# One DMA queue for loads and stores of a batched matmul: six batches loaded first, then stores and loads in turns of two

## The chip, the cores and the metric

The kernel runs on one core of a Trainium2 chip. The metric is the time of one execution in device microseconds (us). The runs of one comparison were made on one chip, in alternating rounds. A ratio is the mean time of one kernel's runs over that of the other's runs of the same rounds, so it is not quite the ratio of the medians that stand beside it.

## The reference

```python
# x: 16 x 768 x 512, y: 16 x 768 x 1024, float32
def reference(x, y):
    return np.einsum('bkm,bkn->bmn', x, y).astype(np.float32)
```

For each of 16 batches, 1.573 MB of x and 3.146 MB of y come in and 2.097 MB go out. That is 109.05 MB in all, each byte moved once.

## The kernel before

SyncE issues every transfer on one queue. Two staging buffers (`xs`, `ys`) take a batch's x and y as float32. VectorE casts them to bf16 (`xb`, `yb`), TensorE multiplies into two halves of PSUM, and ScalarE copies the result into one of five output buffers (`ob`), from which it is stored. The order on the queue is the matter of this document:

```python
    LAG = 4
    NO = 5
    ...
    def store(b):
        if b < B - 2:
            nc.sync.wait_ge(groups, 2 * (b + 2))       # TensorE has finished batch b + 1
        else:
            nc.sync.wait_ge(outs, b - (B - 3))         # ScalarE has copied batch b
        nc.sync.dma_start(o_v[b], ob[b % NO][:]).then_inc(so[b % NO], 16)

    for b in range(B):
        i = b % 2
        if b >= 2:
            nc.sync.wait_ge(cast, nx[b - 2])           # xs[i] has been cast
        wide_dma("x", xs[i][:], x_v[b], 4, True).then_inc(sx[i], 16)
        if b >= 2:
            nc.sync.wait_ge(cast, nx[b - 2] + parts(b - 2))   # ys[i] has been cast
        wide_dma("y", ys[i][:], y_v[b], 2, True).then_inc(sy[i], 16)
        if b >= LAG:
            store(b - LAG)
    for b in range(B - LAG, B - 1):
        store(b)
    ...
    # ScalarE, before it copies batch b into ob[b % NO]:
        if b >= NO:
            nc.scalar.wait_ge(so[b % NO], 16 * (b // NO))     # store b - 5 has landed
    ...
    nc.sync.dma_start(o_v[B - 1], ob[(B - 1) % NO][:])        # the last store, after the section
```

(Comments added; the rest is cut.) Below, x5, y5 and S5 are batch 5's loads and its store. The order of before is x0 y0 ... x4 y4, S0, x5 y5, S1, x6 y6, and so on to y15, S11, and then S12 to S15. I call a move from loads into stores a switch (turn or excursion); before has 12, the last of them into the stores that end the program.

Of the kernel before, what the change touches and what calls it, by code (L numbers as in the profile page):

```python
# [1 line left out]

_os.environ.setdefault("NEURON_RT_ULTRASERVER_MODE", "4")

# [2 lines left out]

# [5 lines left out]


@with_exitstack
def kernel(
    ctx: ExitStack,
    tc: tile.TileContext,
    x: bass.AP,
    y: bass.AP,  # L20
    out: bass.AP,
):
    nc = tc.nc
    P = 128
    FP32 = mybir.dt.float32
    BF16 = mybir.dt.bfloat16

    B, K, M = x.shape
    _, _, N = y.shape
    KT = K // P  # L30
    MT = M // P
    NF = 512
    NT = N // NF



    x_v = x.rearrange("b (p ko) m -> b p ko m", ko=KT)
    y_v = y.rearrange("b (p ko) n -> b p ko n", ko=KT)
    o_v = out.rearrange("b (p mo) n -> b p mo n", mo=MT)

    LAG = 4
    NO = 5
    KH = KT // 2

    section = ExitStack()
    section.enter_context(tc.tile_critical())
    ec = ctx.enter_context
    xs = [ec(nc.sbuf_tensor(f"xs{i}", [P, KT, M], FP32)) for i in range(2)]
    ys = [ec(nc.sbuf_tensor(f"ys{i}", [P, KT, N], FP32)) for i in range(2)]
    xb = ec(nc.sbuf_tensor("xb", [P, 2, KT, M], BF16))  # L50
    yb = ec(nc.sbuf_tensor("yb", [P, 2, KT, N], BF16))
    ob = [ec(nc.sbuf_tensor(f"ob{i}", [P, MT, N], FP32)) for i in range(NO)]

    HB = MT // 2
    ps = [ec(nc.psum_tensor(f"ps{i}", [P, HB, NT, NF], FP32)) for i in range(2)]
    sx = [ec(nc.semaphore(f"sx{i}")) for i in range(2)]
    sy = [ec(nc.semaphore(f"sy{i}")) for i in range(2)]
    so = [ec(nc.semaphore(f"so{i}")) for i in range(NO)]
    cast = ec(nc.semaphore("cast"))
    ready = ec(nc.semaphore("ready"))  # L60
    room = ec(nc.semaphore("room"))
    groups = ec(nc.semaphore("groups"))
    idle = ec(nc.semaphore("idle"))
    outs = ec(nc.semaphore("outs"))


    made = {}

    def wide_dma(key, dst, src, dram_rows, load):


        if key not in made:
            made[key] = nc.sync.dma_start(dst, src)
            return made[key]
        pat = mybir.BassSymbolicTensorAccessPattern
        widen = lambda a: a.rearrange("(q r) k m -> q (r k m)", r=dram_rows)
        plain = lambda a: a.rearrange("p k m -> p (k m)")
        s, d = (widen(src), plain(dst)) if load else (plain(src), widen(dst))
        return nc.sync.add_instruction(_copy.replace(
            made[key].ins, name=nc.get_next_instruction_name(),  # L80
            ins=(pat(ap=s.ap, dtype=s.dtype, bass_ap=s, is_dma=False),),
            outs=(pat(ap=d.ap, dtype=d.dtype, bass_ap=d, is_dma=False),),
            sync_info=None, ant_dge_precooked=False))


    def parts(b):
        return 2 if b in (15,) else 1


    nx = [sum(1 + parts(a) for a in range(b)) + 1 for b in range(B)]  # L90


    def store(b):


        if b < B - 2:
            nc.sync.wait_ge(groups, 2 * (b + 2))
        else:
            nc.sync.wait_ge(outs, b - (B - 3))
        nc.sync.dma_start(o_v[b], ob[b % NO][:]).then_inc(so[b % NO], 16)  # L100

    for b in range(B):
        i = b % 2
        if b >= 2:
            nc.sync.wait_ge(cast, nx[b - 2])
        wide_dma("x", xs[i][:], x_v[b], 4, True).then_inc(sx[i], 16)
        if b >= 2:
            nc.sync.wait_ge(cast, nx[b - 2] + parts(b - 2))
        wide_dma("y", ys[i][:], y_v[b], 2, True).then_inc(sy[i], 16)
        if b >= LAG:  # L110
            store(b - LAG)
    for b in range(B - LAG, B - 1):
        store(b)


    for _ in range(60):
        nc.vector.sem_inc(idle, 1)
    for b in range(B):
        i = b % 2
        n = 16 * (b // 2 + 1)  # L120
        if b >= 2:
            nc.vector.wait_ge(groups, 2 * (b - 1))
        nc.vector.wait_ge(sx[i], n)
        nc.vector.tensor_copy(xb[:, i], xs[i][:]).then_inc(cast, 1)  # L124
        nc.vector.wait_ge(sy[i], n)
        for h in range(parts(b)):
            ks = slice(h * KT // parts(b), (h + 1) * KT // parts(b))
            nc.vector.tensor_copy(yb[:, i, ks], ys[i][:, ks]).then_inc(cast, 1)  # L128


    for b in range(B):
        nc.gpsimd.wait_ge(cast, nx[b]).then_inc(ready, 1)
        for h in range(parts(b)):
            nc.gpsimd.wait_ge(cast, nx[b] + h + 1).then_inc(ready, 2 // parts(b))


    x_w = xb[:].rearrange("p s k (j mo) -> p s k mo j", mo=MT)
    pe = OrderedEngineSet([nc.tensor.engine])
    with nc.Fori(0, B // 2, engines=pe):
        with nc.Fori(0, 2, engines=pe) as s:  # L140
            nc.tensor.wait_ge(ready, 2).then_inc(ready, -2)
            for mo in range(MT):
                g, m = divmod(mo, HB)
                if m == 0:
                    nc.tensor.wait_ge(room, 1).then_inc(room, -1)  # L145
                for kt in range(KT):
                    if mo == 0 and kt == KH:
                        nc.tensor.wait_ge(ready, 1).then_inc(ready, -1)
                    for nt in range(NT):
                        mm = nc.tensor.matmul(  # L150
                            ps[g][:, m, nt], x_w[:, bass.ds(s, 1), kt, mo],
                            yb[:, bass.ds(s, 1), kt, nt * NF:(nt + 1) * NF],
                            start=(kt == 0), stop=(kt == KT - 1))
                if m == HB - 1:
                    mm.then_inc(groups, 1)


    nc.scalar.nop().then_inc(room, 2)
    for _ in range(60):
        nc.scalar.sem_inc(idle, 1)  # L160
    for b in range(B):
        if b >= NO:
            nc.scalar.wait_ge(so[b % NO], 16 * (b // NO))
        for g in range(2):
            nc.scalar.wait_ge(groups, 2 * b + g + 1)
            cp = nc.scalar.copy(ob[b % NO][:, g * HB:(g + 1) * HB].rearrange("p m (t f) -> p m t f", f=NF),  # L166
                                ps[g][:])
            if b < B - 1:
                cp.then_inc(room, 1)
        if b == B - 2:  # L170
            nc.scalar.drain().then_inc(outs, 1)
    cp.then_inc(outs, 1)

    for b in range(B - LAG - 1, B - 2):
        nc.sync.wait_ge(so[b % NO], 16 * (b // NO + 1))
    section.close()




    nc.sync.dma_start(o_v[B - 1], ob[(B - 1) % NO][:])


# [1 line left out]
_INS = ['x', 'y']  # L185
_OUTS = [((16, 512, 1024), 'float32')]


# [23 lines left out]
```

## Time and profile before

| | before |
|---|---|
| time, median of the first 3 runs | 261.9 us (261.72 to 262.05) |
| span in the profile | 260.7 us |
| busiest compute engine | TensorE, 71% |
| queue: share of 16 engines' span | 98.1% |
| bytes over span | 418 GB/s |

The profile's page gives busy time as a share of the span, and a row of 40 equal slices in tenths. Here the row "DMA" is the one that matters, since it stands at 8 or 9 nearly throughout. Where a load landed is best read from VectorE in the timeline: its cast of y starts as soon as the y load's semaphore is full. The columns of such a line are start (us), duration (us), engine, source line, operation, tiles, shapes, and in brackets the idle time ahead and what ended it. The prediction shows these lines.

### The profile page before, as it was taken

How to read it: one execution, taken by the hardware profiler on the slowest of the kernel's cores; microseconds unless marked ns; L12 is line 12 of the kernel's file. 1: busy time of each engine (PE TensorE's matmuls, PEld its weight loads, DVE VectorE, ACT ScalarE, POOL GpSimd, SP SyncE). 2: the span in 40 equal slices, each digit the busy share in tenths (PEclk: the TensorE clock that was granted, in tenths of full speed). 3: DMA queues.
4: the chain of work that ended last, by engine and by line, in shares of the span. 5: the costliest groups of instructions: out<-in, count | busy, mean ns of one | idle time of the engine just before them, and what ended most of it. 6: DMA issues, size and time to landing. Idle time of an engine off the chain costs nothing. (4 is left out here: it accounts for less than half of the span.)

```text
span 260.7 us, 2506 instructions
## 1 busy us (share of the span) xinstructions
PE 186.1 (71%) x768; PEld 89.8 (34%) x768; DVE 82.0 (31%) x33; ACT 61.1 (23%) x33; POOL 0.2 (0%) x4
## 2 busy tenths in 40 slices
PE   0009999998937949479596894969959197696910
PEld 0004555554512515124242351434425043253500
DVE  0261644525222252312524115252142522225000
ACT  1000442243220222202214022040322205022220
POOL 0000000000000000000000000000000000000000
PEclk9999999999995999959889797797999889799985
DMA  7998999999899899989999989999998999999994
GB/s 260 432 494 385 468 385 468 392 392 488 385 410 493 370 450 475 427 385 405 483 400 437 465 367 453 410 483 402 410 485 382 445 468 417 410 410 430 427 410 181
DMA packets 4514, 109.07 MB, mean 418 GB/s; under 512 B 768, under 2 KB 768, under 8 KB 768
## 3 DMA queue, kind: packets, MB, share of 16 engines
q1 hardware_dynamic: 4512, 109.05, 98.1%
q14 instruction: 2, 0.02, 0.0%
HBM read 75.50 MB, written 33.55 MB: 418 GB/s over the span
## 5 line engine op out<-in xcount | busy, mean ns | idle before, releaser
L150 PE MATMUL ps<-yb,xb 128*128 x768 | 186.1, 407 | 62.7 <-PEq L145 60.7
L150 PEld LDWEIGHTS ps<-yb,xb 128*128 x768 | 89.8, 117 | 158.5 <-issue 92.2
L166 ACT COPY ob<-ps 128x2048 f32<-128x2048 f32 x32 | 59.8, 1870 | 184.2 <-PE ps L150 184.2
L128 DVE CAST yb<-ys 128x6144 bf16<-128x6144 f32 (+1 forms) x17 | 53.8, 3171 | 87.7 <-DMA ys<-in_y_dram 87.7
L124 DVE CAST xb<-xs 128x3072 bf16<-128x3072 f32 x16 | 28.2, 1760 | 69.4 <-DMA xs<-in_x_dram 65.3
L166 ACT ACT_TABLE_LOAD x1 | 1.3, 1283 | 5.3 <-issue 5.3
L196 POOL MEMSET const-bfloat16-1.0<- 128x1 bf16 x1 | 0.1, 102 | 0.0
L196 POOL MEMSET const-uint8-127<- 128x1 uint8 x1 | 0.1, 102 | 0.0
L196 POOL MEMSET const-float32-1.0<- 128x1 f32 x1 | 0.1, 99 | 0.0
L196 POOL MEMSET const-float32-0.0<- 128x1 f32 x1 | 0.1, 98 | 0.2 <-issue 0.2
## 6 DMA issues: line engine op xcount, KB each, us to landing
ys<-in_y_dram SPq DMA_DIRECT2D x16, 3072.0 KB, 28.2
out_dram<-ob SPq DMA_DIRECT2D x16, 2048.0 KB, 32.6
xs<-in_x_dram SPq DMA_DIRECT2D x16, 1536.0 KB, 29.7
```

Source lines behind the costliest of these rows:

```text
L124: nc.vector.tensor_copy(xb[:, i], xs[i][:]).then_inc(cast, 1)
L128: nc.vector.tensor_copy(yb[:, i, ks], ys[i][:, ks]).then_inc(cast, 1)
L150: mm = nc.tensor.matmul(ps[g][:, m, nt], x_w[:, bass.ds(s, 1), kt, mo], yb[:, bass.ds(s, 1), kt, nt * NF:(nt + 1) * NF], start=(kt == 0), ...
L166: cp = nc.scalar.copy(ob[b % NO][:, g * HB:(g + 1) * HB].rearrange("p m (t f) -> p m t f", f=NF), ps[g][:])
L196: nc = _bacc.Bacc("TRN2", target_bir_lowering=False, num_devices=1)
```

## The change

It is meant to alternate less often between reading and writing the memory, and to have more loads ahead of the compute engines at the start. Six batches are loaded before the first store. Then two stores and two loads take turns.

```diff
-    LAG = 4
+    FIRST = 6
+    TURN = 2
     NO = 5
...
-    for b in range(B):
+    def load(b):
         i = b % 2
         ...            # x and y of batch b, with the same waits
-        if b >= LAG:
-            store(b - LAG)
-    for b in range(B - LAG, B - 1):
+
+    for b in range(B):
+        load(b)
+        if b + 1 >= FIRST and (b + 1 - FIRST) % TURN == 0:
+            a = b + 1 - FIRST
+            for c in range(a, a + TURN):
+                store(c)
+    for b in range(B - FIRST + TURN, B - 1):
         store(b)
...
-    for b in range(B - LAG - 1, B - 2):
+    for b in range(B - NO, B - 2):      # the same range, 11 to 13
         nc.sync.wait_ge(so[b % NO], 16 * (b // NO + 1))
```

The order is then x0 y0 ... x5 y5, S0 S1, x6 y6 x7 y7, S2 S3, ..., x14 y14 x15 y15, S10 S11, S12 to S15: 6 switches, 5 of them among the loads.

## The prediction

> **What bounds the kernel now.** I read the page first, then the queue's own waits, then VectorE's line in the timeline, because VectorE starts a cast as soon as a load has landed and so marks the landings.
>
> ```profile
> span 260.7 us, 2506 instructions
> PE 186.1 (71%) x768; PEld 89.8 (34%) x768; DVE 82.0 (31%) x33; ACT 61.1 (23%) x33; POOL 0.2 (0%) x4
> ...
> DMA  7998999999899899989999989999998999999994
> ...
> q1 hardware_dynamic: 4512, 109.05, 98.1%
> ...
> PE 9%; ACT 1%; issue 0%
> ...
> ys<-in_y_dram SPq DMA_DIRECT2D x16, 3072.0 KB, 28.2
> out_dram<-ob SPq DMA_DIRECT2D x16, 2048.0 KB, 32.6
> xs<-in_x_dram SPq DMA_DIRECT2D x16, 1536.0 KB, 29.7
> ```
>
> No compute engine is over 71%. The one queue is busy 98.1% of the span, in nearly every slice. The chain that ended last accounts for only 10% of the span: it follows instructions and stops where a transfer is the releaser, so it is no guide here. A transfer of 2 to 3 MB needs some 5 to 7 us but lands 28 to 33 us after its issue: about 21 to 28 us of it is standing in line behind others. The queue is never short of work in the steady part.
>
> The queue's own waits (where the issuing engine stands still):
>
> ```profile
> SPq L73 <- DVE yb L128: 117.0, 14, 9.1
> SPq L73 <- DVE xb L124: 66.7, 14, 6.0
> SPq L100 <- PE ps L150: 28.2, 4, 15.9
> ```
>
> The issuer waits 184 us for casts that free the two staging buffers. That looks like a bound and isn't one: with 28 us between issue and landing, these waits run while earlier transfers move.
>
> VectorE in the timeline; a line with "yb<-ys" starts where a batch's y has landed (first column, us):
>
> ```profile
> 26.19 3.36 DVE L128 CAST yb<-ys 128x6144 bf16<-128x6144 f32 x1 [5.54 <-DMA ys<-in_y_dram]
> ...
> 37.18 3.36 DVE L128 CAST yb<-ys 128x6144 bf16<-128x6144 f32 x1 [3.86 <-DMA ys<-in_y_dram]
> ...
> 48.18 3.36 DVE L128 CAST yb<-ys 128x6144 bf16<-128x6144 f32 x1 [4.49 <-DMA ys<-in_y_dram]
> ...
> 188.27 3.36 DVE L128 CAST yb<-ys 128x6144 bf16<-128x6144 f32 x1 [5.45 <-DMA ys<-in_y_dram]
> 196.85 1.76 DVE L124 CAST xb<-xs 128x3072 bf16<-128x3072 f32 x1 [5.23 <-DMA xs<-in_x_dram]
> 204.06 3.36 DVE L128 CAST yb<-ys 128x6144 bf16<-128x6144 f32 x1 [5.45 <-DMA ys<-in_y_dram]
> ...
> 219.89 3.36 DVE L128 CAST yb<-ys 128x6144 bf16<-128x6144 f32 x1 [5.46 <-DMA ys<-in_y_dram]
> 228.48 1.76 DVE L124 CAST xb<-xs 128x3072 bf16<-128x3072 f32 x1 [5.23 <-DMA xs<-in_x_dram]
> 235.70 3.43 DVE L128 CAST yb<-ys 128x3072 bf16<-128x3072 f32 x2 [5.46 <-DMA ys<-in_y_dram]
> ```
>
> Three readings. (1) From an x landing to its y landing lie 7.21 us (196.85 to 204.06): 3.146 MB at 436 GB/s. (2) Batches 1 to 3 come with no store among them: 10.99 and 11.00 us for 4.719 MB. (3) Batches 12 to 15 come with one store each: 15.79, 15.83 and 15.81 us, mean 15.81, for 6.816 MB. The difference, 15.81 less 11.00, is 4.81 us for the 2.097 MB of a store: again 436 GB/s. **A store put between two loads costs its own bytes and nothing for the turn from reading to writing and back.**
>
> **What the Trainium skill says.** "DMA: Bandwidth & Descriptors", section "Where 436 GB/s comes from", gives 16 ports x 32 B x 850 MHz = 435.2 GB/s as the ceiling of the core's path; the trace agrees (436 in readings 1 and 3). The same page, section "Two DMAs through the same engine are not ordered", says that descriptors of one queue start in order but are pipelined, and that an engine's read and write sides are separate queues. That fits a turn that costs nothing: the next descriptor need not wait for the last to be written. "HBM Reference", section "Access", puts a core that streams alone at about 425 GB/s, bounded by its 16 DMA engines; here 418 is the mean over the span with its start and end. No page I read gives a cost for alternating loads and stores.
>
> **The change part by part.** The bytes stay: 16 x (1.573 + 3.146 + 2.097) = 109.05 MB, at 436 GB/s 250.2 us. The last store was issued at 250.88 and landed after 9.0 us (the minimum among the stores), at 259.9: 9.7 us above the floor. Where those lie, from landing less bytes so far over 436 GB/s: 4.5 us at batch 1 (start-up and first latency), 4.9 at batch 3, 8.2 at batch 8 (124.86 less 116.7), 9.5 at batch 15. So 4.5 us belong to the start, 3.3 came between batches 3 and 8, and the rest is 0.17 us a batch, which is in the store-free batches too (11.00 less 10.83), so it isn't a turn.
>
> Turns: before, stores 0 to 10 lie singly among the loads, 11 excursions. After, stores 0 to 9 lie in five pairs: six excursions fewer. By the difference of readings 2 and 3 each is worth 4.81 - 2.097/0.436 = 0.00 us, and the spread of the steady batches is 0.04 us. Gain: 6 x 0.00, at most 6 x 0.04 = 0.2 us. If I charged the whole 0.17 us to the turn, 1.0 us.
>
> Loads early: y4 and x5 are issued as before, since each waits for the cast two batches back (y5 at 48.18 + 3.36 = 51.5, as now). Store 0 now moves behind y5 rather than ahead of x5. So y5 should land 4.8 us earlier than its present 76.28, near 71.3, and the stores 0 and 1 about 76 and 81. The queue doesn't run dry: y5 is cast at about 74.8 and y7 issued then, while most of store 0, store 1, x6, y6 and x7 (together 9.6 + 3.6 + 7.2 + 3.6 = 24 us of bytes) are still ahead of it. In the pairs that follow, between a y and the y that takes its buffer lie two x, one y and two stores, 10.5 MB or 24 us, as now; the cast and issue take about 4.
>
> Output buffers: ScalarE's copy for an odd batch b now needs store b-5, which stands directly behind y of batch b. It lands 4.8 us after that y. ScalarE needs it after the cast (3.4) and half of TensorE's batch (5.2, the spacing of the copies in the timeline), 8.6 us after that y. Slack 3.8 us, no wait.
>
> Tail: after y15 now come stores 10 to 15 rather than 11 to 15. y15 should land 4.8 us earlier, near 230.9. Behind it are 6 x 4.81 = 28.9 us of stores: 259.8, where the end is now. Store 15 must be issued some 2 us before store 14 has moved (about 255). TensorE takes batch 14 from 223.8 as now (y14 has the same bytes ahead of it), ends it near 236, goes straight on with 15 (before, it began at 238.03) and ends near 247; ScalarE's copy near 249, and the issue comes after store 13's landing near 250. In time; and a last store issued sooner is worth nothing while store 14 is still moving.
>
> Sum: turns 0 to -0.2, loads early 0, buffers 0, tail 0.
>
> **The rivals.** A: turns are dear. Then the pairs save up to the 1.0 us above (260.9), and if all that slipped after batch 3 (4.6 us) were due to alternation, halving it would give 2.3 us: 259.6. Against it: the 0.7 us lost between y3 (48.18) and y4 (59.71) fell before any store had moved; the steady batches lose nothing. B: a new wait. Bunched stores could let the staging buffers starve or ScalarE stall on an output buffer, each pair then opening a hole of 1 to 2 us in the queue, five times: 267 to 272. For it: the slack for the odd batches is 3.8 us, where before a store stood a whole batch ahead of its reuse. Against it: the 28 us of standing in line, and that a late ScalarE first eats into TensorE's idle time (62.7 us), not the queue's. C: the irregular losses, 3.3 us between batches 3 and 8, move. They have no cause that the views show, and a different order of reads and writes meets them differently: about 1 us either way. D: the tail with compute on the path. Were y15's compute what sets the end, 4.8 us would be saved; but the stores behind it move at full rate to the end, so the earlier landing is paid back in full by the extra store behind it.
>
> **Range and chances.** I predict 261.8 us: the 261.9 of before less 0.1. The spread of before is 0.3 us; rival C gives about 1 us either way, A up to 2 us down, B is unlikely. Range 260.3 to 263.2. Faster by 2% means below 256.7: it would take all of the 4.6 us that slip after batch 3 and more; 2 in 100. Slower by 2% means above 267.1: rival B in each pair; 4 in 100. Within 2%: 94 in 100.
>
> **What would show it.** Right: the queue's busy share stays near 98%; from one odd batch's y landing to the next odd one's about 31.6 us (twice 15.81), with 11.0 us inside a pair and 20.6 across two stores; y15's cast begins near 231 rather than 235.7; the last store is issued near 250 and the span ends near 260.6. Wrong by A: less than 31.4 us for a pair of batches, and an end before 259. Wrong by B: slices of DMA below 9 in the middle, ScalarE waiting for a store, stores landing much later than 38 us after issue. Wrong by D: an end that follows y15's landing down.

## The result, and the profile after

| | before | after |
|---|---|---|
| median, 4 runs each | 261.98 us (261.72 to 262.17) | 261.6 us (261.33 to 261.67) |
| ratio, after over before | | 0.9984, 95% interval 0.9967 to 1.0002 |
| span in the profile | 260.7 us | 259.9 us |

The verdict is "same", and the range on record held it. The page of the changed kernel has the same picture as before:

```profile
span 259.9 us, 2506 instructions
...
DMA  7998999999999998999999999999999999999994
...
q1 hardware_dynamic: 4512, 109.05, 98.3%
...
ys<-in_y_dram SPq DMA_DIRECT2D x16, 3072.0 KB, 28.3
out_dram<-ob SPq DMA_DIRECT2D x16, 2048.0 KB, 32.7
xs<-in_x_dram SPq DMA_DIRECT2D x16, 1536.0 KB, 29.8
```

The queue's share rose from 98.1% to 98.3%, and the times from issue to landing (last column, us) moved by 0.1 us each. The queue was full before and is full after. VectorE's casts of y in the timeline of the changed kernel show the new rhythm:

```profile
25.89 3.36 DVE L135 CAST yb<-ys 128x6144 bf16<-128x6144 f32 x1 [5.54 <-DMA ys<-in_y_dram]
...
58.87 3.36 DVE L135 CAST yb<-ys 128x6144 bf16<-128x6144 f32 x1 [4.53 <-DMA ys<-in_y_dram]
...
70.48 3.36 DVE L135 CAST yb<-ys 128x6144 bf16<-128x6144 f32 x1 [5.78 <-DMA ys<-in_y_dram]
...
91.21 3.36 DVE L135 CAST yb<-ys 128x6144 bf16<-128x6144 f32 x1 [5.48 <-DMA ys<-in_y_dram]
...
102.20 3.36 DVE L135 CAST yb<-ys 128x6144 bf16<-128x6144 f32 x1 [5.47 <-DMA ys<-in_y_dram]
...
122.87 3.36 DVE L135 CAST yb<-ys 128x6144 bf16<-128x6144 f32 x1 [5.47 <-DMA ys<-in_y_dram]
...
133.86 3.36 DVE L135 CAST yb<-ys 128x6144 bf16<-128x6144 f32 x1 [5.47 <-DMA ys<-in_y_dram]
...
229.42 3.43 DVE L135 CAST yb<-ys 128x3072 bf16<-128x3072 f32 x2 [5.47 <-DMA ys<-in_y_dram]
```

These are y1, y4 to y9, and y15. Inside a pair, y6 to y7, lie 10.99 us; across two stores, y7 to y8, lie 20.67 us, of which 20.67 - 10.99 = 9.68 us, or 4.84 each, belong to the stores. y15 is cast at 229.42, not 235.70: 6.3 us earlier. The end came only 0.8 us earlier. One more store stands behind y15, which takes back 4.8 us, and the stretch from y15's cast to the end took 0.7 us more beyond its stores (25.0 us for five stores before, 30.5 us for six after). The last issues of the two kernels, in the timeline of SyncE, before and after:

```profile
250.88 0.33 SPq L181 DMA_DIRECT2D out_dram<-ob  x1
```

```profile
249.97 0.33 SPq L188 DMA_DIRECT2D out_dram<-ob  x1
```

Two lines of detail bear on what was wrong in the prediction. In before, y4 and y5 were cast at these times:

```profile
59.71 3.36 DVE L128 CAST yb<-ys 128x6144 bf16<-128x6144 f32 x1 [5.67 <-DMA ys<-in_y_dram]
...
76.28 3.36 DVE L128 CAST yb<-ys 128x6144 bf16<-128x6144 f32 x1 [6.18 <-DMA ys<-in_y_dram]
```

Before, y3 to y4 took 59.71 - 48.18 = 11.53 us, 0.54 more than the 10.99 of a batch without a store. After, it took 10.99, and y4 to y5 took 70.48 - 58.87 = 11.61. The long step moved with the first store. y4 before and y5 after are each the load just ahead of it. In the records of single DMA packets, the first packet of S0 began at 57.7 us in before, 2.0 us ahead of y4's cast, and at 68.9 in after, 1.6 us ahead of y5's. So the long load was still under way when the first store began.

**A measure for the experiments.** Two steady figures, 10.99 us for a batch's loads and 15.81 - 10.99 = 4.82 us for a store, account for a queue that loses nothing. (The 4.82 us includes a switch, but stores in longer rows cost no less: 4.84 us each in rows of two, above, and in the rows of three and four below. So a settled switch costs nothing that shows.) I call slip what the stretch from y1's cast to y15's takes beyond 14 x 10.99 + 4.82 for each store that stands ahead of y15. For before: 235.70 - 26.19 - 153.86 - 11 x 4.82 = 2.6 us. For after: 229.42 - 25.89 - 153.86 - 10 x 4.82 = 1.5 us. If switches cost nothing anywhere, slip has no reason to depend on the order. Slip ends at y15, so what is lost behind y15 is not in it.

**Where the slip sits.** The records of single DMA packets in the trace also show it. Each transfer ends with 16 completion writes, one for each DMA engine. Their times for the first load and the last store, in us, worked out from those records:

```
                    first load: earliest, latest    last store: earliest, median, latest
before                   6.3     6.9                    256.6   256.7   259.5
after                    6.1     6.8                    256.2   256.8   258.6
```

Most of the 16 engines end together. In before three end 0.8 to 1.4 us behind the median and one 2.8 us; in after the last two end 1.3 and 1.8 us behind it. A transfer counts as landed only when the last has written. The lag grows on the way: the last write came 0.8 us behind the median at y1 and 3.0 at y15 in before, 0.6 and 1.3 in after. In before, the records that ran long are nearly all packets of a y load just ahead of a store: 0.2 to 0.7 us long on nearly all engines at the first switch, later mainly on the engine that lags (0.8, 0.7 and 0.6 us at three of the next four switches) and less on the others. So what the change could touch is the long load at the first switch and the lag of the slowest engine.

### The profile page after: what moved, and what is told of

It is laid out like the page before. It is cut to its first block, busy times and chain, and to the rows that moved or that the text cites. A ratio compares the mean times of both kernels' runs of the same rounds, so it can differ in the third digit from the quotient of the medians.

```text
span 259.9 us, 2506 instructions
## 1 busy us (share of the span) xinstructions
PE 178.8 (69%) x768; PEld 88.8 (34%) x768; DVE 82.0 (32%) x33; ACT 61.1 (24%) x33; POOL 0.2 (0%) x4
## 3 DMA queue, kind: packets, MB, share of 16 engines
q1 hardware_dynamic: 4512, 109.05, 98.3%
## 5 line engine op out<-in xcount | busy, mean ns | idle before, releaser
L157 PE MATMUL ps<-yb,xb 128*128 x768 | 178.8, 397 | 65.8 <-PEq L152 65.8
L157 PEld LDWEIGHTS ps<-yb,xb 128*128 x768 | 88.8, 116 | 155.4 <-issue 84.0
L173 ACT COPY ob<-ps 128x2048 f32<-128x2048 f32 x32 | 59.8, 1870 | 180.1 <-PE ps L157 180.1
```

Source lines behind the costliest of these rows:

```text
L157: mm = nc.tensor.matmul(ps[g][:, m, nt], x_w[:, bass.ds(s, 1), kt, mo], yb[:, bass.ds(s, 1), kt, nt * NF:(nt + 1) * NF], start=(kt == 0), ...
L173: cp = nc.scalar.copy(ob[b % NO][:, g * HB:(g + 1) * HB].rearrange("p m (t f) -> p m t f", f=NF), ps[g][:])
```

## The experiments

The theory (theory 1): the queue is always full, switches are free, the bytes set the time. Its rivals: switches cost (theory 2), or the new order starves ScalarE or the buffers (rival B). Seven kernels, and the change once more, ran on one chip; four runs that those results led to followed on another. All results were correct except those of the two kernels that do no compute. Medians of before were 261.97, 262.52 and 262.23 us.

### One part alone: six loads first, stores singly

```diff
-    LAG = 4
+    LAG = 5
```

> The six loads come first, then stores singly: the change without its pairs (10 excursions into stores among the loads, where before has 11 and the pairs have 5). Theory 1, of the prediction: turns are free and the queue is full throughout, so within 0.3 us of before (261.6 to 262.3) and y15 is cast near 230. Theory 2, formed from the two traces: the last y ahead of a store is lengthened, by 0.5 to 0.6 us at the first turn and by little or nothing later. Then the long step moves to y5: y3 to y4 takes 11.0 us (11.53 before), y4 to y5 about 11.6, as in the kernel with pairs; the time is 261.7 to 262.1. Rival B (ScalarE or buffers starve with the store so close to its reuse): over 263.

Measured: 261.74 us, ratio to before 0.9992 (0.9979 to 1.0005). y15 was cast at 229.82. y3 to y4 took 11.00 and y4 to y5 11.86 us, so the long step moved to the load ahead of the first store, as expected of theory 2. The slip was 1.8 us. Rival B has no support: ScalarE waited for no store. The early loads, with one store fewer ahead of y15, are worth nothing that the interval can tell from zero.

### Fewer switches: three by three

```diff
-    FIRST = 6
-    TURN = 2
+    FIRST = 7
+    TURN = 3
```

> Seven loads first, then three stores and three loads in turns: 3 excursions among the loads instead of 5 or 11. With five output buffers ScalarE must now wait for stores (batch 5 needs store 0, which stands behind y6). Theory 1: ScalarE and TensorE wait up to 7 us per turn, but from idle time, the queue never runs dry, turns are free: 261.3 to 262.0. Theory 2 (turns cost a little): 0.1 to 0.3 us below the pairs, 261.2 to 261.6. Rival B: the new ScalarE waits reach the queue; over 263.

Measured: 260.84 us, ratio 0.9957 (0.9945 to 0.9970); on the other chip, below, 0.9952. This is lower than any theory had it. The slip fell to 0.6 us. The waits show at the same time that ScalarE now stands still for stores (columns: us in all, times, longest):

```profile
ACT ob L173 <- PE ps L157: 141.7, 24, 20.3
...
ACT ob L173 <- DMA out_dram<-ob: 35.5, 4, 10.8
```

35.5 us of new waiting, and the kernel is faster. The waits replace idle time that ScalarE spent on TensorE (180.1 us in the changed kernel, 141.7 here). Rival B's mechanism exists and doesn't reach the queue.

### Halves of stores, together and apart

The control issues the two halves of each of stores 0 to 14 one after the other; the test puts one half behind x and one behind y.

```diff
-        nc.sync.dma_start(o_v[b], ob[b % NO][:]).then_inc(so[b % NO], 16)
+        for h in range(2):
+            nc.sync.dma_start(o_v[b][:, 2 * h:2 * h + 2],
+                              ob[b % NO][:, 2 * h:2 * h + 2]).then_inc(so[b % NO], 16)
...            # the waits on so count 32 for a store, not 16
```

> Each of stores 0 to 14 of the kernel before is issued as two halves one right after the other: the same 11 excursions, with packets of 8 KB instead of 16 KB. It is the control for the next run. A packet of 8 KB took 307 to 309 ns in the trace of before and one of 16 KB 611, so 16 engines' share grows by some 15 x 8 x 5 ns = 0.6 us at most plus the extra completion writes: 262.0 to 262.9 under each theory.

Measured: 262.53 us, ratio to before 1.0023 (1.0010 to 1.0036): the price of smaller packets, within what was expected (two packets of 8 KB took 2 x 309 ns in this trace, where one of 16 KB took 611 in before). The test, shown against the control:

```diff
         wide_dma("x", xs[i][:], x_v[b], 4, True).then_inc(sx[i], 16)
+        if b >= LAG:
+            store(b - LAG, (0,))
         if b >= 2:
             nc.sync.wait_ge(cast, nx[b - 2] + parts(b - 2))
         wide_dma("y", ys[i][:], y_v[b], 2, True).then_inc(sy[i], 16)
         if b >= LAG:
-            store(b - LAG)
+            store(b - LAG, (1,))
...            # store() takes the halves to issue as an argument
```

> The same halves, but one behind x and one behind y: 23 excursions instead of 11 or 12. Against the control of halves issued together. Theory 1 (turns free): within 0.3 us of that control. Theory 2 (a turn costs a little, 0.05 to 0.2 us each on the slowest of the 16 engines): 0.5 to 2 us above it. Rival A (0.17 us a turn in full): about 2 us above it. If the turn costs only after a y load and not after an x load: as theory 1.

Measured: 261.68 us, ratio to before 0.9995 (0.9981 to 1.0010), so 0.85 us below its control by the medians, where every theory had it level or above. Twice as many switches cost nothing; they even went with less slip (1.6 against 2.6 us, by the same measure). A fixed price per switch, theory 2 as I had put it, is refuted by this pair. Of the 1.6 us, 1.3 came at the first switch (y3 to y4 took 14.67 us, where 10.99 and half a store make 13.40); the 22 later switches took 0.3.

### The changed kernel again

> The changed kernel once more, in five rounds against before on this chip. Each theory: 0.1 to 0.6 us below before. If the difference is only which engine happened to be hit in one trace, it goes to zero; if turns cost, it stays near 0.4 us.

Measured: 261.85 us against 262.52 of before in the same rounds, ratio 0.9974 (0.9961 to 0.9986). The gain is small but clear of zero here. This trace's slip was 2.0 us, against 1.5 in the first, so single traces of one kernel differ by half a microsecond.

### No compute

TensorE's and ScalarE's work is taken out, and the five output buffers are filled with zeros once. VectorE still casts and so still paces the loads.

```diff
-        if b < B - 2:
-            nc.sync.wait_ge(groups, 2 * (b + 2))
-        else:
-            nc.sync.wait_ge(outs, b - (B - 3))
+        nc.sync.wait_ge(outs, NO)
...
-        if b >= 2:
-            nc.vector.wait_ge(groups, 2 * (b - 1))
...            # all of TensorE's and ScalarE's loops removed
+    for t in ob:
+        nc.gpsimd.memset(t[:], 0.0).then_inc(outs, 1)
```

> Wrong results on purpose: TensorE and ScalarE do nothing, the stores write zeros from buffers filled once, VectorE casts as before and paces the loads; order of the kernel before. Theory 1: the queue alone sets the time, so 261 to 262, and the batch steps are those of before (11.0 us without a store, 15.8 with one). If the slips between batches 3 and 8 come from compute that uses the on-chip memory beside the transfers: they vanish and the time falls by 2 to 3 us to 259 or 260.

Measured: 262.19 us, ratio to before 0.9992 (0.9979 to 1.0005). Without any matmul the kernel takes the same time, which is the plainest proof that, in this order, the queue alone sets it. The slip is there too, 2.5 us; y3, y4 and y5 in VectorE's timeline of this kernel:

```profile
48.02 3.36 DVE L123 CAST yb<-ys 128x6144 bf16<-128x6144 f32 x1 [5.54 <-DMA ys<-in_y_dram]
...
59.74 3.36 DVE L123 CAST yb<-ys 128x6144 bf16<-128x6144 f32 x1 [6.27 <-DMA ys<-in_y_dram]
...
75.61 3.36 DVE L123 CAST yb<-ys 128x6144 bf16<-128x6144 f32 x1 [5.56 <-DMA ys<-in_y_dram]
```

59.74 - 48.02 = 11.72 us: the long step ahead of the first store needs no TensorE or ScalarE beside it.

> The same without compute in the order of the changed kernel. Theory 1 (turns free): as the one before, within 0.2 us. Theory 2 (turns cost on the slowest engine): 0.3 to 0.6 us below it, as with compute. If the small gain of the pairs comes from compute moved in time, there is none here.

Measured: 261.21 us, ratio to before 0.9952 (0.9938 to 0.9965); by the medians 1.0 us below the run without compute in the order of before, more than expected. Its slip was 1.9 us. So the small gain of the pairs is there without compute, and belongs to the transfers. With compute the pairs took 261.85 us in the same rounds, 0.6 more than without: in this order compute costs a little after all, and no run here shows where.

### The other direction: four loads first

```diff
-    LAG = 4
+    LAG = 3
...
-    for b in range(B - LAG - 1, B - 2):
+    for b in range(B - NO, B - 2):
```

> The opposite direction: single stores, begun one load earlier (12 excursions among the loads). y15 has one more store ahead of it and should land 4.8 us later, near 240.5. From y15's landing to the issue of the last store before took 15.2 us (235.70 to 250.88), so it is issued near 255.7 and lands 7 to 9 us after, while store 14 ahead of it has moved by 255: compute comes onto the path and the time is 264 to 266. If the queue alone set the end (theory 1 taken without its limit): 262. Theory 2 on the first turn: the long step moves to y3: y2 to y3 about 11.5 us, y3 to y4 15.8 as it has a store.

Measured: 264.56 us, ratio 1.0076 (1.0063 to 1.0089), as expected. y2 to y3 took 11.81 us: the long step moved to the load ahead of the first store once more. At the end the queue ran dry, which the row of slices shows (last but one, 4 tenths), beside the last cast of y and the last issue:

```profile
DMA  7998999999989989999999989989999999998947
```

```profile
240.91 3.43 DVE L128 CAST yb<-ys 128x3072 bf16<-128x3072 f32 x2 [5.44 <-DMA ys<-in_y_dram]
```

```profile
256.06 0.33 SPq L181 DMA_DIRECT2D out_dram<-ob  x1
```

y15 to the last issue takes 15.2 us in both orders (235.70 to 250.88 before, 240.91 to 256.06 here). Before has four stores behind y15 to fill that time, S11 to S14, 19.3 us; here there are three, 14.5 us, and a hole of up to 4 us opened on the DMA engines ahead of the last store.

### A store behind x instead of y

```diff
         wide_dma("x", xs[i][:], x_v[b], 4, True).then_inc(sx[i], 16)
+        if b >= LAG:
+            store(b - LAG)
         if b >= 2:
             nc.sync.wait_ge(cast, nx[b - 2] + parts(b - 2))
         wide_dma("y", ys[i][:], y_v[b], 2, True).then_inc(sy[i], 16)
-        if b >= LAG:
-            store(b - LAG)
```

> The order of before, but each store stands between a batch's x and its y rather than behind y: as many excursions (12), each after an x load. In the halves issued apart, half of the excursions followed an x, there were twice as many, and it was faster than the halves together by 0.85 us. Theory 3: what costs is the switch after a y load, on one or two of the 16 engines that lag; after an x load it costs little but for the first. Then 260.6 to 261.3, 0.7 to 1.3 us below before. Theory 2 (every switch costs alike): 261.7 to 262.3, as before. If it was the smaller store that helped, not its place: as before too.

Measured: 265.03 us, ratio 1.0103 (1.0079 to 1.0127). The expectation had overlooked that S11 now stands ahead of y15: y15 was cast at 239.94, the last store issued at 256.59, and the tail was exposed as with four loads first. The time therefore says nothing of theory 3. The slip still does: 2.3 us with 12 stores ahead, no less than before's 2.6 by more than single traces differ. Theory 3, that a switch behind y is the dear one, has no support here. The batch of the first switch, behind x4, took 1.3 us of the 2.3; the other 11 switches took 0.95, where those behind a y load took 0.9 (six first), 2.1 (before) and 2.4 (four first). Single traces spread too widely to tell.

### Three by three again, threes behind x, four by four

> The fastest so far, again and on this chip: 1.1 us (0.4%) below before if the gain is its own; ScalarE waits on stores again some 35 us in 4 waits.

Measured: 260.86 us, ratio 0.9952 (0.9939 to 0.9964); slip 0.7 us; ScalarE waited 37.4 us for stores. The gain holds on a second chip.

The next takes the three by three and moves its first three turns between a batch's x and its y, leaving the last behind y15.

```diff
     def load(b):
         ...
         wide_dma("x", xs[i][:], x_v[b], 4, True).then_inc(sx[i], 16)
+        if b < B - 1:
+            turn(b)          # the three stores that are due after load b
         ...
     for b in range(B):
         load(b)
-        ...                  # the turn after both loads
+    turn(B - 1)
```

> Both together: three stores at a time, and the first three turns behind an x load; the last stays behind y15. Theory 3: 0.2 to 0.5 us below the three by three. If the number of turns alone counts: equal to it within 0.2 us.

Measured: 260.98 us, ratio 0.9955 (0.9943 to 0.9968): equal to the three by three. The stores behind y15 are the same in both, so this is the clean comparison that the run before failed to be, and it shows none of the gain that theory 3 forecast. The slip was 1.2 us, of which 1.1 came at the first switch, behind x6: the three by three had 0.1 to 0.4 there, behind y6. ScalarE waited 13.4 us for stores.

```diff
-    FIRST = 6
-    TURN = 2
+    FIRST = 8
+    TURN = 4
```

> Eight loads first, then four stores and four loads in turns: 2 excursions among the loads, and ScalarE waits longer for stores with the same five output buffers. If fewer turns keep paying: 0.1 to 0.4 us below the three by three. If the waits reach TensorE's last batches, the last store is issued after 250.5 and the time is 0.5 to 3 us above it.

Measured: 260.52 us, ratio 0.9941 (0.9928 to 0.9954), the fastest of all. The slip was 0.4 us, and ScalarE waited 60.3 us for stores. The casts of y1 and y15, and the last issue, which was later than in before (250.88) and in the three by three (249.16):

```profile
25.87 3.36 DVE L135 CAST yb<-ys 128x6144 bf16<-128x6144 f32 x1 [5.54 <-DMA ys<-in_y_dram]
...
218.69 3.43 DVE L135 CAST yb<-ys 128x3072 bf16<-128x3072 f32 x2 [4.69 <-DMA ys<-in_y_dram]
```

```profile
251.18 0.33 SPq L188 DMA_DIRECT2D out_dram<-ob  x1
```

The last store's 16 completion writes came between 256.9 and 257.4 us: no engine lags, and even the earliest ends 0.3 us later than in before. Between 251 and 252 us the DMA engines were busy for a share of only 0.43 (0.85 in before), while the last store was awaited. Part of the gain is thus spent on a last store that is issued late. With 0.4 us of slip left, I estimate that longer turns have little more to win; no run tried them.

### The runs side by side

Switches are counted among the loads, without the one into the final stores. Slip is from each run's single profile; the ratio is to before.

| order | switches | slip, us | ratio |
|---|---|---|---|
| four first, single | 12 | 3.2 | 1.0076 (tail exposed) |
| store behind x | 12 | 2.3 | 1.0103 (tail exposed) |
| before | 11 | 2.6 | 1 |
| no compute, order of before | 11 | 2.5 | 0.9992 |
| six first, single | 10 | 1.8 | 0.9992 |
| the change | 5 | 1.5 and 2.0 | 0.9984 and 0.9974 |
| no compute, order of the change | 5 | 1.9 | 0.9952 |
| three by three | 3 | 0.6 and 0.7 | 0.9957 and 0.9952 |
| threes behind x | 3 | 1.2 | 0.9955 |
| four by four | 2 | 0.4 | 0.9941 |
| halves together | 11 | 2.6 | 1.0023 (smaller packets) |
| halves apart | 23 | 1.6 | 0.9995 (smaller packets) |

Among orders of whole stores, fewer and longer turns go with less slip on the whole, though 10 switches (1.8) and 5 (1.5 and 2.0) can't be told apart. The packet records say the same of the slowest engine: its lag behind the median at y15 was 3.0 us in before, 1.3 and 2.4 in the two traces of the change, 0.8 in both of the three by three and 0.6 in the four by four. The times gain less than the slips: the four by four has 2.2 us less slip than before and is about 1.6 us faster, since some is lost again behind y15. One rival is not separated: with longer turns the first store also comes later and fewer stores stand ahead of y15 (11 in before, 8 in the four by four). The six first moves these by one only, and no run kept eight loads first with single stores. The halves show that the count of switches alone is not the law. What it is that makes an engine lag, and why halves apart lag less, I leave open: no run here shows it.

## Why the prediction was right

**The bound.** Shown. The queue was full before and after, and taking all of TensorE's and ScalarE's work away changed the time by 0.1% in the order of before and 0.2% in that of the change. The long waits of SyncE for casts cost nothing, as read.

**Turns at 0.00 us.** This step was too small, and the range held because the whole term is small beside it. It was taken from batches 12 to 15 of before, the settled end of the run, where a store does cost its bytes alone. The slips lie earlier, and the prediction had set these aside as of no visible cause, partly with the argument that the step from y3 to y4 slipped "before any store had moved". That argument is refuted: the long step moved to y3, y4, y5 or later with the first store, and S0's first packets had begun 2.0 us ahead of y4's cast. So it belongs to the load just ahead of the first store. The term "turns 0 to -0.2" measured about -0.4 us in the first comparison (not clear of zero) and -0.7 in the second (clear of it). How much of that the fewer switches bring, and how much the early loads, is not shown. The prediction's rival A (up to 2.3 us down) was in part right, at about a sixth to a third of that size. The signs that it named for A, less than 31.4 us for a pair of settled batches and an end before 259, could not see it: they stood at 31.66 and 259.9.

**The 0.17 us a batch that "isn't a turn".** Right that it isn't, but it isn't a loss either. The 436 GB/s came from x's cast to y's cast, two different waits; a whole batch of loads takes 10.99 us, 429 GB/s, in every kernel here, and that is the rate to use.

**Loads early, buffers.** Right. y5 was cast at 70.48 (71.3 predicted; its own sum, 76.28 - 4.8, gives 71.5). A pair of batches took 31.66 us from y7 to y9 (31.6 predicted), with 10.99 inside and 20.67 across. ScalarE waited for no store in the changed kernel, and no store took over 36.7 us to land. Rival B's waits came about in the threes and the four by four alone, and cost mostly idle time: only in the four by four is the last store issued later than in before.

**The tail.** Right, and now with its edge. y15 came 6.3 us earlier, where 4.8 were forecast (1.1 us is less slip, 0.3 us an earlier start), and the end gained 0.8, as said above. The last issue near 250 was 249.97. Rival D is refuted by the changed kernel, and its reverse is shown by four loads first: one store fewer behind y15, and the 15.2 us of compute behind y15 come onto the path.

**Rival C.** Of its 1 us either way, half a microsecond shows between two traces of one kernel. That the slips have no cause in the order was wrong. (Of the sums: the 9.5 us at batch 15 should be 9.6, 235.70 less 98.57 MB at 436 GB/s. The figure of 425 GB/s stands in the section "Specifications (TRN2)" of its page.)

## What to carry to other kernels

Where one queue is full from start to end, as here, first work out what there is to win: here the slip, 2.6 us of 261, of which the best order won about 1.6. Read the cost of a switch from the whole run, the first switch above all, not from the settled batches alone. And at the end of a kernel, keep enough stores behind the last load to cover the compute that follows it: here 15.2 us against 4.8 us a store, so at least four. Before had four, and its engines dipped only to 0.85 for a microsecond.

## What the Trainium skill lacked or had wrong

- "DMA: Bandwidth & Descriptors" gives no figure for loads and stores that alternate on one queue. Here a settled alternation cost nothing (a store alone between loads took 4.82 us, one in a row of two to four 4.84), the load ahead of the first store ran 0.1 to 0.9 us long with whole stores behind a y load, and the stretch from y1 to y15 lost 2.6 us with 11 switches, 0.4 with two.
- The same page, section "Latency and other measured facts", puts slower engines down, as a best guess, to descriptor rings that only software-generated transfers use. Here all transfers came from SyncE's queue, and the last of the 16 engines still ended 2.8 us behind the median in before (256.7 and 259.5) and 1.8 in after. The records don't give the engines' numbers, so whether they are the page's 7 and 15 is open.
- The same page, section "Bandwidth", gives 425 GB/s for a 16 MB load, issued from GpSimd. Loads issued from SyncE held 429 GB/s here (4.719 MB in 10.99 us) and whole kernels 414 to 422 GB/s over their spans, start and end included; its ceiling of 435.2 GB/s was never held over a whole batch.
